# A hybrid encoder's RWKV-7 layer: gate weights scaled earlier, chunk matrices of all key tiles ahead of the gate products, and the triangular substitution started beside them

## The chip, the cores and the metric

The kernel runs on one core of one Trainium2 chip. The metric is the device time of one execution in microseconds, the median of several runs. A core has five engines with instruction streams of their own: TensorE (PE, with weight loads as PEld), VectorE (DVE), ScalarE (ACT), GpSimd (POOL) and SyncE (SP, which here issues the DMA transfers). They wait for one another by semaphores, and each runs its own stream in order.

## What is computed

The reference is a trunk of two layers over one sequence of 512 tokens with 1024 features. Layer 0 mixes tokens by a short gated convolution, layer 1 by RWKV-7; each is followed by a squared-ReLU MLP, with RMS norms and a modulation by a conditioning vector. The change lies in the RWKV-7 mixer:

```
xr, xw, xk, xv, xa, xg = h[None] + xx[None] * mu[:, None, None, :]
r, k, v = jnp.einsum('nbsd,nde->nbse', jnp.stack([xr, xk, xv]), w_rkv)
w = -jax.nn.softplus(-(w0 + jnp.tanh(xw @ w1) @ w2)) - 0.5
a = jax.nn.sigmoid(a0 + (xa @ a1) @ a2)
g = jax.nn.sigmoid(xg @ g1) @ g2
kk = heads(k * k_k)
kk = kk / jnp.maximum(jnp.sqrt(jnp.sum(kk * kk, axis=-1, keepdims=True)), 1e-12)
k = k * (1 + (a - 1) * k_a)
decay = jnp.exp(-jnp.exp(heads(w)))
y = _wkv7_scan(rh, decay, kh, vh, -kk, kk * ah)
...
out = ((y + bonus).reshape(bsz, seq, d).astype(h.dtype) * g) @ w_o
```

The scan runs token by token in the reference. The kernel cuts the sequence into chunks of 64 tokens; in a chunk the recurrence needs the inverse of a triangular matrix for each head (16 heads, 8 chunks), which is found by substitution.

## The kernel before, in words

Activations are kept transposed, 128 features on the partitions and 512 tokens along the free axis, so the 1024 features make eight tiles (KB). A product with a large weight matrix is done with the weights split into a high and a low part in a narrower format, as three matmuls per block of 128 features (`passes`, L171 to L173), 24 for one output tile. A weight block is loaded by SP (`raw`, L136), cast on ACT (L131), and the rest is subtracted on DVE (L132). DVE, ACT, POOL and SP instructions are put in order by the framework's scheduler; the order of PE is the order in which the code is written (`MANUAL`). In the RWKV layer it is written out as a string, `PLAN` (L34), each letter of which calls a function (`parts`, L833):

- K, `key_tile`: 24 matmuls for one tile of the keys; ACT then copies the tile (L602) and squares it (L604), and the norms' products on PE (L608) are kept back until `f` or a later step. The first three key tiles are done ahead of the plan.
- f: the norms' products that were kept back; n, `norms_now`: root, maximum and reciprocal of the norms so far (L625 to L629).
- W, `second_product`: four matmuls (L683) for the decay and the in-context rate of a tile, with tanh and scaling on ACT (L687 to L689). The prediction calls them decay products.
- s, `scaled`: a running sum of the decay along each chunk on DVE (L715), two exponentials on ACT (L717, L718), the norms repeated over the head's 64 rows by POOL (`repeat_norms`, L620), four transposes of them on PE (L723), and on DVE the scaled vectors (L726, L729, L730, L732, L734), with one product on POOL (L733).
- c, `chunk_matrix`: 16 pairs of small matmuls (L756) of two scaled vectors of the tile, a copy on ACT (L758) and a store to DRAM (L759).
- l: the loads of the gate's first weights (L547, L549) and their scaling on POOL (`gate_scale`, four times L533, one memset L556). L, `gate_lora`: three matmuls of these weights with the normed input (L634, L635, L674). a, G, A: what turns their sum into the gate's input (L793 is its last matmul).
- X, `xr_mix`: one tile of the input of the receptance. B, `chunk_back`: the loads of the chunk matrices (L746) for the substitution. U: the loads of the gate's second weights.

Behind the plan comes a loop of eight r tiles (L1256, 24 matmuls each, with the gates' second products and, in `beside_tile`, L1244, the mixes for the values and the steps of the substitution). The substitution has 30 steps of two DVE operations (L859, L861) over all heads and chunks at once. Its result is stored and read back in another layout by `inverted` (L863), with the tiles of `turn_tiles` (L847) beside it; then come the value tiles and the recurrence over the chunks, whose PE products L966, L982 and L997 wait for copies and products such as L922 (ACT) and L1033 (DVE).

Of the kernel before, what the change touches and what calls it, by code (L numbers as in the profile page):

```python
# [13 lines left out]
ALU = mybir.AluOpType  # L14
# [19 lines left out]
PLAN = "TfffffnWWsKWscfWKscfWscKWscfnWscWUsclscLLcBXXLLXXLLXXLLXXaGA"  # L34
NVEARLY, NTAIL = 2, 2
# [19 lines left out]
def trunk(ctx: ExitStack, tc: tile.TileContext, x_in, vec_in, c_in, ada0, ada, cin_a, wmain,  # L55
# [593 lines left out]
    with tc.manual_schedule(engines=MANUAL):  # L649
# [55 lines left out]
        def scaled():  # L705
# [27 lines left out]
            G.tensor_tensor(m, m, ei, op=ALU.mult)  # L733
# [14 lines left out]
        def chunk_matrix():  # L748
# [10 lines left out]
            nc.sync.dma_start(sc1.rearrange("(j g r) s t -> (r s) j g t", j=KB, r=2)[:, j], ab)  # L759

# [72 lines left out]
        parts = dict(f=lambda: flush(1), K=key_tile, T=first_out, n=norms_now, q=repeat_now,  # L833
# [11 lines left out]
        X2 = Xs[0]  # L845
# [9 lines left out]
        def substitute(t, tm):  # L855
            w = 31 - t
            sh = [P, 2, t, w]
            tv = tm[:, :2 * t * w].rearrange("p (q s c) -> p q s c", q=2, s=t)
            V.tensor_tensor(tv, X2[:, :, :t, t:t + 1].broadcast_to(sh), X2[:, :, t:t + 1, t + 1:].broadcast_to(sh),  # L859
                            op=ALU.mult)  # L860
            V.tensor_tensor(X2[:, :, :t, t + 1:], X2[:, :, :t, t + 1:], tv, op=ALU.add)  # L861

        def inverted():  # L863
            nc.sync.dma_start(sc2.rearrange("q p s t -> p q s t"), X2)
# [370 lines left out]
        for q in range(2):  # L1235
            G.affine_select(out=X2[:, q], in_=X2[:, q], pattern=[[-1, 32], [1, 32]], compare_op=ALU.is_gt, fill=0.0,
                            base=0, channel_multiplier=0)
            G.memset(X2[:, q].rearrange("p s t -> p (s t)")[:, 0:1024:33], 1.0)
        work = lambda t: 150 + 2 * t * (31 - t)
        steps, tm = list(range(30, 0, -1)), tmp()  # L1240
        total, subst = [sum(map(work, steps))], [0]
        nr = KB - done["R"]

        def beside_tile(i, mixes):  # L1244
            while len(xv) < mixes:
                xv.append(pair())
                mix(3, len(xv) - 1, FULL, *xv[-1])
            while steps and subst[0] + work(steps[0]) / 2 < total[0] * (i + 1) / (nr + NVEARLY - NTAIL):
                t = steps.pop(0)
                substitute(t, tm)  # L1250
                subst[0] += work(t)
                if not steps:
                    inverted()

        side = chain(*(v_tile(j) for j in range(KB)), x_back(), o_part(0), o_part(1), o_part(2))
        for i in range(nr):  # L1256
# [7 lines left out]
            if i == nr - 1:  # L1264
                turn_tiles()
# [113 lines left out]
```

## Time and profile before

| what | value |
|---|---|
| median of 3 runs | 1392.74 us (1389.88 to 1393.55) |
| profiled execution | 1391.49 us |
| its span in the trace | 1389.8 us |
| mean granted PE clock | 0.966 |
| PE busy | 1316.7 us (95%) |
| DVE busy | 838.3 us (60%) |
| ACT busy | 553.7 us (40%) |
| POOL busy | 163.2 us (12%) |

The durations in this document come from the profiled execution; its span is what the trace covers, and the execution's own time is 1.7 us longer. Shares of busy time are means over a program with many stages; the change concerns the stretch from about 625 us, where the plan begins, to about 806 us, where the recurrence over the chunks has begun. A wait in the profile is the idle time of an engine ahead of an instruction, put down to the instruction that released it. For a group of instructions in one row, the time is that of the group.

### The profile page before, as it was taken

How to read it: one execution, taken by the hardware profiler on the slowest of the kernel's cores; microseconds unless marked ns; L12 is line 12 of the kernel's file. 1: busy time of each engine (PE TensorE's matmuls, PEld its weight loads, DVE VectorE, ACT ScalarE, POOL GpSimd, SP SyncE). 2: the span in 40 equal slices, each digit the busy share in tenths (PEclk: the TensorE clock that was granted, in tenths of full speed). 3: DMA queues.
4: the chain of work that ended last, by engine and by line, in shares of the span. 5: the costliest groups of instructions: out<-in, count | busy, mean ns of one | idle time of the engine just before them, and what ended most of it. 6: DMA issues, size and time to landing. Idle time of an engine off the chain costs nothing.

```text
span 1389.8 us, 20232 instructions
## 1 busy us (share of the span) xinstructions
PE 1316.7 (95%) x8182; PEld 1080.1 (78%) x8182; DVE 838.3 (60%) x1233; ACT 553.7 (40%) x943; POOL 163.2 (12%) x175
## 2 busy tenths in 40 slices
PE   6899999999999999899599899999889999999997
PEld 3688889888888888887458677776678888888886
DVE  6996667756747565727669735465584344343445
ACT  3243334323233234547554557674344232232331
POOL 2300020000000003513311123232310000000000
PEclk7999999999999999998799999999999999999999
DMA  8466532635636355202445603321122223222231
GB/s 326 147 230 251 185 121 107 247 132 195 244 137 257 135 191 188 107 16 69 152 76 185 151 30 116 122 101 39 47 91 74 93 93 105 91 101 96 91 107 61
DMA packets 83392, 184.44 MB, mean 133 GB/s; under 512 B 35329, under 2 KB 37633, under 8 KB 83298
## 3 DMA queue, kind: packets, MB, share of 16 engines
q1 hardware_dynamic: 83298, 183.14, 38.6%
q8 instruction: 64, 1.05, 0.3%
q14 instruction: 30, 0.25, 0.1%
HBM read 168.44 MB, written 13.63 MB: 131 GB/s over the span
## 4 chain that ended last, share of the span: by engine, by line
PE 45%; ACT 3%; DVE 2%; issue 1%; POOL 0%; DVEq 0%; ACTq 0%
PE ps L171 12%; PE ps L173 12%; PE ps L172 11%; PE ps L982 1%; ACT b L1004 1%; PE ps L1060 1%; PE ps L1027 1%; PE ps L1096 1%; PE ps L1079 1%; PE ps L634 1%; PE ps L635 1%; PE ps L1091 1%; PE ps L674 0%; PE ps L1016 0%; PE ps L1120 0%
## 5 line engine op out<-in xcount | busy, mean ns | idle before, releaser
L171 PE MATMUL ps<-b,w 128*128 128x512 f32 (+1 forms) x1486 | 573.6, 386 | 1.2 <-ACT w L131 0.7
L173 PE MATMUL ps<-b,w 128*128 128x512 f32 (+1 forms) x1486 | 566.1, 381 | 2.2 <-POOL w L132 1.3
L172 PE MATMUL ps<-b,w 128*128 128x512 f32 (+1 forms) x1486 | 566.5, 381 | 0.0
L131 ACT CAST w<-raw 128x1024 fp32r<-128x1024 f32 x176 | 185.1, 1053 | 460.5 <-PE ps L172 432.1
L171 PEld LDWEIGHTS ps<-b,w 128*128 128x128 f32 x1486 | 282.7, 190 | 57.6 <-issue 3.2
L173 PEld LDWEIGHTS ps<-b,w 128*128 128x128 f32 x1486 | 282.7, 190 | 56.1 <-POOL w L132 1.8
L172 PEld LDWEIGHTS ps<-b,w 128*128 128x128 f32 x1486 | 282.8, 190 | 49.7
L132 DVE TENSOR_TENSOR w<-raw,w 128x1024 fp32r<-128x1024 f32 x172 | 211.8, 1232 | 144.5 <-ACT w L131 139.4
L205 DVE CUSTOM_DVE_ANT_0 cj<-b,cj,vec 128x1024 f32<-128x1024 f32 x96 | 137.9, 1436 | 10.8 <-DMA b<-in_ada 10.3
L302 DVE SCALAR_TENSOR_TENSOR b<-ps,mod,b 128x512 f32<-128x512 f32 (+1 forms) x84 | 56.4, 672 | 121.6 <-PE ps L173 121.2
L131 ACT CAST b<-t 128x512 fp32r<-128x512 f32 (+1 forms) x113 | 66.2, 591 | 114.3 <-DVE t L347 80.9
L132 DVE TENSOR_TENSOR b<-t,b 128x512 fp32r<-128x512 f32 x97 | 66.4, 692 | 26.7 <-ACT b L131 26.6
L302 DVE SCALAR_TENSOR_TENSOR xy<-ps,mod,xy 128x512 f32<-128x512 f32 x32 | 24.0, 750 | 62.1 <-PE ps L173 62.1
L256 ACT ACTIVATE b<-t,mod 128x256 fp32r<-128x256 f32 (+2 forms) x56 | 29.4, 537 | 56.0 <-DVE t L255 51.6
L171 PE MATMUL ps<-b,b 128*128 128x256 f32 (+1 forms) x152 | 47.3, 318 | 1.2 <-ACT b L256 1.1
L347 DVE TENSOR_TENSOR t<-t 128x512 f32<-128x512 f32 x64 | 43.5, 685 | 7.3 <-ACT t L346 7.3
L433 PE MATMUL ps<-b,b 128*128 128x512 f32 x168 | 40.6, 396 | 6.9 <-ACT b L256 6.9
L231 DVE TENSOR_TENSOR t<-t,t 128x256 f32<-128x256 f32 (+1 forms) x47 | 41.7, 886 | 7.8 <-ACT t L230 7.1
L172 PE MATMUL ps<-b,b 128*128 128x256 f32 (+1 forms) x152 | 45.0, 297 | 0.6 <-POOL b L132 0.6
L173 PE MATMUL ps<-b,b 128*128 128x256 f32 (+1 forms) x152 | 44.7, 295 | 0.0
L433 PEld LDWEIGHTS ps<-b,b 128*128 128x128 f32 x168 | 30.9, 188 | 16.9 <-ACT b L256 10.6
L533 POOL TENSOR_TENSOR b<-b,vec 128x512 f32<-128x512 f32 (+2 forms) x4 | 4.7, 1195 | 325.5 <-DMA b<-in_l 323.9
(208 smaller groups left out, 1321.3 us busy)
## 6 DMA issues: line engine op xcount, KB each, us to landing
raw<-in_wmain SPq DMA_DIRECT2D x185, 512.0 KB, 3.3
b<-in_ada SPq DMA_DIRECT2D x96, 512.0 KB, 5.7
sp<-b SPq DMA_DIRECT2D x8, 512.0 KB, 2.7
b<-sp SPq DMA_DIRECT2D x8, 512.0 KB, 4.6
b<-in_cin_a SPq DMA_DIRECT2D x8, 448.0 KB, 6.9
b<-in_x SPq DMA_DIRECT2D x8, 256.0 KB, 6.1
xs<-b SPq DMA_DIRECT2D x8, 256.0 KB, 2.3
sc<-t SPq DMA_DIRECT2D x8, 256.0 KB, 2.8
```

Source lines behind the costliest of these rows:

```text
L131: A.copy(dst_hi, src)
L132: return (eng or V).tensor_tensor(dst_lo, src, dst_hi.bitcast(F32), op=ALU.subtract)
L171: PE.matmul(dst, whi, ahi, start=start, stop=False)
L172: PE.matmul(dst, whi, alo, start=False, stop=False)
L173: return PE.matmul(dst, wlo, ahi, start=False, stop=stop)
L205: return V.tensor_tensor_reduce(junk, w, cb, 1.0, vv(f"ab{l}{v}", m), ALU.mult, ALU.add, mods[l, v][:, m:m + 1])
L231: V.tensor_tensor(acc[:, sl], acc[:, sl], t[:, :w], op=ALU.add)
L256: A.activation(hi[:, sl], t[:, :w], AF.Identity, bias=sh[:, k:k + 1])
L302: V.scalar_tensor_tensor(x[m][:, sl], pt[:, sl], gt[:, m:m + 1], x[m][:, sl], op0=ALU.mult, op1=ALU.add)
L347: V.tensor_tensor(r, r, r, op=ALU.mult)
L433: PE.matmul(pts[i], a[:, i * P:(i + 1) * P], h[k][b], start=k == 0 and a is whi and not b, stop=k == KB - 1 and b == 1)
L634: PE.matmul(pt[:, sl], w0, h[k][:, sl], start=start, stop=False)
```

## The change

In the plan, the loads and the scaling of the gate weights (l) stand first; the norms (f) stand right behind their key tile; each tile's chunk matrix (c) stands behind its own scaled step (s), with all eight ahead of the first gate product (L); and a new letter u runs steps of the substitution (a share of 0.06 of its work each) between the gate products. The product L733 goes from POOL to DVE. What is left of the substitution is spread over the first seven r tiles instead of the first eight, the store of its result is issued right behind its last step, and the tiles that are read back, and the reading, come behind the r loop.

```diff
--- before.py
+++ after.py
@@ -31,8 +31,8 @@
 POSTW = 0.742
 STATY = 0.155
 BENG = None
-PLAN = "TfffffnWWsKWscfWKscfWscKWscfnWscWUsclscLLcBXXLLXXLLXXLLXXaGA"
-NVEARLY, NTAIL = 2, 2
+PLAN = "TlfffffnWWsWsKfcWscWsKfcWscKfncWscWsUcscLLBXXLXXLXXLuXXLuLLuaGAu"
+NVEARLY, NSUB, USUB = 2, 7, 0.06
 G2ENG = None
 NMORE = 2
 TA = (0, 1), (0, 1), (0, 1)
@@ -730,7 +730,7 @@
             V.scalar_tensor_tensor(bt, al, -0.5, bt, op0=ALU.mult, op1=ALU.mult)
             al3 = al.rearrange("p (c t) -> p c t", t=64)
             V.tensor_tensor(al3[:, :, 1:], al3[:, :, 1:], e3[:, :, :63], op=ALU.mult)
-            G.tensor_tensor(m, m, ei, op=ALU.mult)
+            V.tensor_tensor(m, m, ei, op=ALU.mult)
             V.tensor_tensor(kt, kt, m, op=ALU.mult)
 
         Xs = []
@@ -757,6 +757,33 @@
             ab = tmp().rearrange("p (c t) -> p c t", t=64)
             A.copy(ab, pab)
             nc.sync.dma_start(sc1.rearrange("(j g r) s t -> (r s) j g t", j=KB, r=2)[:, j], ab)
+
+
+        work = lambda t: 150 + 2 * t * (31 - t)
+        steps, tms = list(range(30, 0, -1)), []
+        total, subst = sum(map(work, steps)), [0.0]
+
+        def substitute(t):
+            X2, tm = Xs[0], tms[0]
+            w = 31 - t
+            sh = [P, 2, t, w]
+            tv = tm[:, :2 * t * w].rearrange("p (q s c) -> p q s c", q=2, s=t)
+            V.tensor_tensor(tv, X2[:, :, :t, t:t + 1].broadcast_to(sh), X2[:, :, t:t + 1, t + 1:].broadcast_to(sh),
+                            op=ALU.mult)
+            V.tensor_tensor(X2[:, :, :t, t + 1:], X2[:, :, :t, t + 1:], tv, op=ALU.add)
+
+        def advance(part):
+            if not tms:
+                tms.append(tmp())
+                for q in range(2):
+                    X = Xs[0][:, q]
+                    G.affine_select(out=X, in_=X, pattern=[[-1, 32], [1, 32]], compare_op=ALU.is_gt, fill=0.0, base=0,
+                                    channel_multiplier=0)
+                    G.memset(X.rearrange("p s t -> p (s t)")[:, 0:1024:33], 1.0)
+            while steps and subst[0] + work(steps[0]) / 2 / total < part:
+                t = steps.pop(0)
+                substitute(t)
+                subst[0] += work(t) / total
 
         g2, gahl = [], []
 
@@ -830,7 +857,7 @@
             A.copy(gt_, pg)
             nc.sync.dma_start(gs[:, j], gt_)
 
-        parts = dict(f=lambda: flush(1), K=key_tile, T=first_out, n=norms_now, q=repeat_now,
+        parts = dict(u=lambda: advance(subst[0] + USUB), f=lambda: flush(1), K=key_tile, T=first_out, n=norms_now, q=repeat_now,
                      W=second_product, L=gate_lora, X=xr_mix, l=lambda: (gate_loads(), gate_scale()), U=gate_loads2, G=gate_weights, a=gate_part, A=gate_in, s=scaled, c=chunk_matrix,
                      R=r_tile, p=spill, g=gates, b=lambda: chunk_back(1),
                      B=lambda: chunk_back(0), w=lambda: w_raw(wst["nraw"] + 1))
@@ -842,7 +869,6 @@
         TT = []
         s1u = sc1.rearrange("(g u r) s t -> s r g u t", r=2, g=4)
         s2u = sc2.rearrange("q (g u r) s t -> q s r g u t", r=2, g=4)
-        X2 = Xs[0]
 
         def turn_tiles():
             TT.extend(big((P, 16, 64), F32) for _ in range(4))
@@ -852,16 +878,8 @@
                     G.memset(TT[g][o + 32:o + 64, :, 0:32], 0.0)
                     nc.sync.dma_start(TT[g][o:o + 32, :, 32:], s1u[0:32, par, g, :, 32:])
 
-        def substitute(t, tm):
-            w = 31 - t
-            sh = [P, 2, t, w]
-            tv = tm[:, :2 * t * w].rearrange("p (q s c) -> p q s c", q=2, s=t)
-            V.tensor_tensor(tv, X2[:, :, :t, t:t + 1].broadcast_to(sh), X2[:, :, t:t + 1, t + 1:].broadcast_to(sh),
-                            op=ALU.mult)
-            V.tensor_tensor(X2[:, :, :t, t + 1:], X2[:, :, :t, t + 1:], tv, op=ALU.add)
-
         def inverted():
-            nc.sync.dma_start(sc2.rearrange("q p s t -> p q s t"), X2)
+            turn_tiles()
             for g in range(4):
                 for q in range(2):
                     for par in range(2):
@@ -1232,25 +1250,16 @@
             yield XWAIT
 
 
-        for q in range(2):
-            G.affine_select(out=X2[:, q], in_=X2[:, q], pattern=[[-1, 32], [1, 32]], compare_op=ALU.is_gt, fill=0.0,
-                            base=0, channel_multiplier=0)
-            G.memset(X2[:, q].rearrange("p s t -> p (s t)")[:, 0:1024:33], 1.0)
-        work = lambda t: 150 + 2 * t * (31 - t)
-        steps, tm = list(range(30, 0, -1)), tmp()
-        total, subst = [sum(map(work, steps))], [0]
-        nr = KB - done["R"]
+        nr, sub0 = KB - done["R"], subst[0]
 
         def beside_tile(i, mixes):
             while len(xv) < mixes:
                 xv.append(pair())
                 mix(3, len(xv) - 1, FULL, *xv[-1])
-            while steps and subst[0] + work(steps[0]) / 2 < total[0] * (i + 1) / (nr + NVEARLY - NTAIL):
-                t = steps.pop(0)
-                substitute(t, tm)
-                subst[0] += work(t)
+            if steps:
+                advance(sub0 + (1 - sub0) * (i + 1) / NSUB)
                 if not steps:
-                    inverted()
+                    nc.sync.dma_start(sc2.rearrange("q p s t -> p q s t"), Xs[0])
 
         side = chain(*(v_tile(j) for j in range(KB)), x_back(), o_part(0), o_part(1), o_part(2))
         for i in range(nr):
@@ -1261,9 +1270,8 @@
             if j < 2:
                 He[j] = big(dt=F32)
                 nc.sync.dma_start(He[j][0:64], ar[j][0:64])
-            if i == nr - 1:
-                turn_tiles()
             beside_tile(i, KB * (i + 1) // nr)
+        inverted()
         for i in range(NVEARLY):
             while len(vdone) <= i:
                 next(side)
```

The orders below are those of one engine's instructions before and in the changed kernel; names such as b, t, ps are buffers with their numbers.

On POOL, at the start of the plan, before (L620 repeats the norms of one tile, L733 is the product of the scaled step):

```order
L620 TENSOR_SCALAR t_4769<-rn 128x512
L620 TENSOR_SCALAR t_4781<-rn 128x512
L733 TENSOR_TENSOR t_4784<-t_4784,t_4772 128x512
L620 TENSOR_SCALAR t_4845<-rn 128x512
L733 TENSOR_TENSOR t_4848<-t_4848,t_4836 128x512
L620 TENSOR_SCALAR t_4933<-rn 128x512
```

and now:

```order
L556 MEMSET b_4729 128x256
L620 TENSOR_SCALAR t_4779<-rn 128x512
L533 TENSOR_TENSOR b_4727<-b_4726,vec 128x1024
L533 TENSOR_TENSOR b_4729<-b_4729,omu 128x8x32
L533 TENSOR_TENSOR b_4726<-b_4726,omu 128x1024
L533 TENSOR_TENSOR b_4729<-b_4729,vec 128x8x32
L620 TENSOR_SCALAR t_4791<-rn 128x512
L620 TENSOR_SCALAR t_4821<-rn 128x512
```

The memset and the four scalings of the gate weights (L556, L533) now stand here, and the second repeated norm (t_4791) stands behind them; L733 has left POOL.

On PE, at the end of the first key tile of the plan (L173 is its last matmul, L608 the products of its norms, L723 the transposes of repeated norms), before:

```order
L173 MATMUL ps_4791<-b_4232,w_4683 128x512
L683 MATMUL ps_4825<-b_4713,b_4029 128x512
L683 MATMUL ps_4825<-b_4713,b_4030 128x512
L683 MATMUL ps_4826<-b_4713,b_4068 128x512
L683 MATMUL ps_4826<-b_4713,b_4069 128x512
L723 MATMUL ps_4840<-ident,t_4781 128x128 x4
L756 MATMUL ps_4855<-b_4755,b_4694 64x64 x16
L608 MATMUL ps_4362<-blk,b_4822 128x2 x4
```

and now:

```order
L173 MATMUL ps_4831<-b_4232,w_4683 128x512
L608 MATMUL ps_4362<-blk,b_4862 128x2 x4
L756 MATMUL ps_4869<-b_4765,b_4694 64x64 x16
L683 MATMUL ps_4889<-b_4713,b_4029 128x512
L683 MATMUL ps_4889<-b_4713,b_4030 128x512
L683 MATMUL ps_4890<-b_4713,b_4068 128x512
L683 MATMUL ps_4890<-b_4713,b_4069 128x512
L723 MATMUL ps_4904<-ident,t_4821 128x128 x4
```

The norms' products moved from behind the decay products, the transposes and the chunk matrix to right behind the key tile. On ACT at the same place (L131 is the cast of a weight block, L602 and L604 are the key tile's copy and square) the cast stands ahead of copy and square, as it did before:

```order
L718 ACTIVATE b_4775<-b_4775 128x512
L720 COPY eend_4714<-b_4775 128x8
L131 CAST w_4994<-raw_4860 128x1024
L602 COPY b_4862<-ps_4831 128x512
L604 ACTIVATE b_4862<-ps_4831,vec 128x512
L758 COPY t_4886<-ps_4869 128x512
```

On PE, from the transposes of the sixth key tile (tile 5) to the first gate product (L634), before:

```order
L723 MATMUL ps_5123<-ident,t_5116 128x128 x4
L756 MATMUL ps_5138<-b_4973,b_4706 64x64 x16
L683 MATMUL ps_5158<-b_4713,b_4029 128x512
L683 MATMUL ps_5158<-b_4713,b_4030 128x512
L683 MATMUL ps_5159<-b_4713,b_4068 128x512
L683 MATMUL ps_5159<-b_4713,b_4069 128x512
L723 MATMUL ps_5179<-ident,t_5128 128x128 x4
L756 MATMUL ps_5194<-b_5057,b_4822 64x64 x16
L723 MATMUL ps_5229<-ident,t_5184 128x128 x4
L756 MATMUL ps_5242<-b_5112,b_4920 64x64 x16
L634 MATMUL ps_5262<-b_4183,b_5214 128x512
```

and now:

```order
L723 MATMUL ps_5153<-ident,t_5146 128x128 x4
L756 MATMUL ps_5168<-b_5033,b_4862 64x64 x16
L683 MATMUL ps_5188<-b_4713,b_4029 128x512
L683 MATMUL ps_5188<-b_4713,b_4030 128x512
L683 MATMUL ps_5189<-b_4713,b_4068 128x512
L683 MATMUL ps_5189<-b_4713,b_4069 128x512
L723 MATMUL ps_5203<-ident,t_5158 128x128 x4
L756 MATMUL ps_5224<-b_5142,b_5000 64x64 x16
L723 MATMUL ps_5249<-ident,t_5208 128x128 x4
L756 MATMUL ps_5262<-b_5194,b_5106 64x64 x16
L634 MATMUL ps_5282<-b_4183,b_4726 128x512
```

Before, the chunk matrices (L756) there were those of tiles 4, 5 and 6, each behind the transposes of the tile after it; now they are those of tiles 5, 6 and 7, each behind the transposes of its own tile.

## Rows read from the trace of the kernel before

**Rows 1.** The table by windows: stretch, length, busy us of each engine, PE clock, DMA

```profile
640.60:642.80 2.20, 2.20 (x7) 1.81 (x7) 2.20 (x3) 0.82 (x3) 1.62 (x2) 0.50 0.45 119
625.08:713.34 88.26, 70.55 (x466) 49.32 (x466) 62.67 (x74) 58.25 (x101) 26.93 (x26) 0.84 0.40 102
778.70:806.40 27.70, 20.13 (x359) 18.61 (x358) 11.70 (x16) 17.69 (x45) 5.59 (x8) 0.82 0.61 154
```

**Rows 2.** Waits of PE from 625 to 714: us in total, times, longest

```profile
PE ps L756 <- DVE b L732: 5.8, 2, 4.3
PE ps L634 <- POOL b L533: 5.7, 1, 5.7
PE ps L723 <- POOL t L620: 2.7, 1, 2.7
PE ps L756 <- ACT b L688: 1.7, 1, 1.7
PE ps L793 <- ACT t L778: 1.3, 1, 1.3
```

**Rows 3.** The timeline of POOL: start us, us, engine, line, operation

```profile
626.33 1.21 POOL L620 TENSOR_SCALAR t<-rn 128x512 f32<-128x512 f32 x2 [26.91 <-PE ps L683]
...
683.52 1.90 POOL L533 TENSOR_TENSOR b<-b,vec 128x1024 f32<-128x1024 f32 x1 [1.59 <-DMA b<-in_g]
685.38 2.91 POOL L533 TENSOR_TENSOR b<-b,omu 128x256 f32<-128x256 f32 x2
688.25 0.61 POOL L533 TENSOR_TENSOR b<-b,vec 128x256 f32<-128x256 f32 x1
```

**Rows 4.** The timeline of SP's DMA issues near 620

```profile
619.81 0.33 SPq L136 DMA_DIRECT2D raw<-in_wmain  x1
```

**Rows 5.** The timeline of ACT behind the second key tile

```profile
648.49 1.05 ACT L131 CAST w<-raw 128x1024 fp32r<-128x1024 f32 x1 [1.73 <-PE ps L172]
649.45 0.58 ACT L602 COPY b<-ps 128x512 f32<-128x512 f32 x1
649.92 0.69 ACT L604 ACTIVATE b<-ps,vec 128x512 f32<-128x512 f32 x1
```

**Rows 6.** The timeline of PE at the same place

```profile
648.29 0.40 PE L173 MATMUL ps<-b,w 128*128 128x512 f32 x1
...
650.67 1.05 PE L608 MATMUL ps<-blk,b 128*128 128x2 f32 x8 [0.46 <-ACT b L604]
```

**Rows 7.** The timeline of DVE, key tiles 5 to 7

```profile
671.88 0.75 DVE L726 SCALAR_TENSOR_TENSOR b<-b,vec,ps 128x512 f32<-128x512 f32 x1 [1.80 <-PE ps L723]
672.54 0.68 DVE L729 SCALAR_TENSOR_TENSOR b<-b,t 128x512 f32<-128x512 f32 x1
673.15 0.68 DVE L734 TENSOR_TENSOR b<-b,t 128x512 f32<-128x512 f32 x1
...
674.54 1.56 DVE L732 TENSOR_TENSOR b<-b 128x504 f32<-128x504 f32 x1
676.02 1.21 DVE L715 TENSOR_TENSOR_SCAN b<-cmask,b 128x512 f32<-128x512 f32 x1
...
679.87 0.68 DVE L732 TENSOR_TENSOR b<-b 128x504 f32<-128x504 f32 x1
...
683.53 2.43 DVE L732 TENSOR_TENSOR b<-b 128x504 f32<-128x504 f32 x1
```

**Rows 8.** The timeline of PE: decay products at the lower and higher clock

```profile
640.68 2.05 PE L683 MATMUL ps<-b,b 128*128 128x512 f32 x4
...
651.58 1.19 PE L683 MATMUL ps<-b,b 128*128 128x512 f32 x4
```

**Rows 9.** Waits from 778 to 807, all engines

```profile
ACT w L131 <- DMA raw<-in_wmain: 9.9, 1, 9.9
...
PEld ps L997 <- ACT b L922: 3.0, 1, 3.0
PE ps L997 <- DVE b L1033: 2.7, 1, 2.7
```

## The prediction

> **What bounds the kernel now.** I read the page first: TensorE (PE) is busy for most of the span, so time is won or lost only where PE stops or runs slowly. Then the table by windows. The change touches the stretch from 625.08 to 713.34, from the end of the first key tiles to the first gate sum. There PE is busy for 70.55 of 88.26 us, with a mean granted clock of 0.84 of full speed; the same table gives 0.82 for the start of the chunk recurrence, where the results of the substitution are first used [rows 1]. These two stretches are where anything can happen. Between them, in the r tiles, the substitution runs on DVE beside a PE that has its weights, so moving its steps there buys nothing by itself.
>
> Then the waits of PE. From 625 to 714 they are 5.8 us for the chunk matrix on the DVE chain (L756 on L732), 5.7 for the first gate product on POOL's scaling of the gate weights (L634 on L533), 2.7 for a transpose on a repeated norm (L723 on L620), 1.7 for a chunk matrix on ACT and 1.3 for the gate sum [rows 2], and 0.46 for the norms' product [rows 6]: **17.7 us of stops**. The change removes the 5.7 at once: the loads and the scaling come before the first remaining key tile. The question is what the new order of PE puts in its place.
>
> **The change part by part.** All sums are against the profiled execution, 1391.49 us, whose span is 1389.8; the median of the runs, 1392.74, is 1.25 above it.
>
> *A: gate weights scaled early.* POOL now holds the first repeated norm, then the four L533, then the second repeated norm. Before, two repeated norms took 1.21 us together from 626.33, 0.61 each; the four L533 took 1.90 + 2.91 + 0.61 = 5.42 [rows 3]. So the second is done at 626.33 + 1.21 + 5.42 = 633.0 at the earliest. The gate loads don't make that later by much: in SP's order they stand right behind a weight load that was issued at 619.81 [rows 4], six microseconds ahead of POOL. PE needs the second repeated norm for the transposes of tile 1, which now stand ahead of the first key tile. It gets there at about 631.3, an estimate: the stretch starts at 625.08, and three decay products (1.19 to 2.05 us each by the clock [rows 8], so 3.6 to 6.2) and the transposes of tile 0 lie ahead; I choose the later end, since the clock is low in a part of them. That makes 1.7 us. But POOL and DVE slow each other here: L732 took 2.43 us while POOL ran its 1.90 us L533, against 0.68 alone, and 1.56 beside a POOL product [rows 7]. DVE runs splits and scans of 1.21 us in the new place (a scan's row: [rows 7]). I take three microseconds of mutual holding, the second repeated norm at 636.0, and a **stop of 4.7 us**; the ends are 1.7 (no holding) and 6.0.
>
> The Trainium skill, page "SBUF — State Buffer", section "Who interferes with whom", says that DVE and GpSimd share one pair of ports under an exclusive lock, held for a whole instruction. It speaks against scaling on POOL in the busiest stretch of DVE; by it the stop would be near 6.0 and the time about 1403.3; by POOL's rows alone it would be 1.7 and the time about 1399.0. L732's 2.43 against 0.68 us agrees with it.
>
> *B: norms right behind the key tile.* Behind a key tile's 24 matmuls come a copy and a square on ACT, and the norms need the square. Before, the second key tile ended at 648.29 + 0.40 = 648.69 [rows 6]. ACT began a weight cast of 1.05 us at 648.49, then copy and square of 0.58 and 0.69; the square began at 649.92 [rows 5], and the norms ran at 650.67, 1.98 us behind the key tile's end, with other products in PE's order between to fill that time, and a wait of 0.46 [rows 6]. Now the norms are PE's next instruction, and the cast still stands ahead of copy and square on ACT. PE stands for about 2.0 us, three times: **6.0 us**. The chunk matrix and the decay product behind the norms don't depend on them, but PE runs in order. The ends are 1.4 (0.46 each, as before) and 6.0.
>
> *C: the chunk matrices of the last tiles.* Before, each of the last tiles' chunk matrices stood behind the transposes of the next tile, and the last one behind gate products, so a tile's DVE chain ran beside the next tile. Now tiles 5, 6 and 7 have their own transposes and their own chunk matrix side by side; the last decay product stands behind tile 5's chunk matrix and covers nothing. The chain from transposes to chunk matrix is L726 (672.54 - 671.88 = 0.66), a scan that the order puts between, 676.02 on (1.21 long, about 1.15 to the next start), four operations of 0.60 each (L729, L733, L730, L734; 673.15 - 672.54 = 0.61 from start to start, and L733 taken like L734, which has its form), and L732 of 0.68 [rows 7]: 0.66 + 1.15 + 2.4 + 0.68 and 0.1 for the two hand-overs (an estimate) = 5.0 for tiles 5 and 6, and about 3.8 for tile 7, which has no scan behind it. **13.8 us**, about what the two old waits on L732, the norm's wait and the wait on L533 were together (5.8 + 5.7 + 2.7 = 14.2). The gate products that are now ready could have filled this, but they come after it in PE's order. Moving L733 from POOL to DVE is in the chain already: one 0.60 more there, and no wait across engines. For the other tiles the key tiles' matmuls cover it. The 2.7 us stop of the transposes on their norm gets a chunk matrix as cover beside the decay product; I count what is left of it at nothing, 0.7 at most.
>
> New stops: 4.7 + 6.0 + 13.8 + 1.3 (the gate sum, unchanged) = 25.8, less 17.7: **+8.1 us**.
>
> *D: the clock.* After a stop PE runs on at the lower of its levels: from 640.60 to 642.80, behind the 1.7 us stop on ACT, the granted clock is 0.50, that is 1.2 GHz, with PE busy all the time [rows 1], and the four decay-product matmuls there take 2.05 us; in the next tile, with no stop ahead, they take 1.19 [rows 8]. The loss of 0.86 on these four is about half of such a stretch (an estimate from these rows): 1.7 us a stop. The change makes four stops among the key tiles (A, and B three times) and removes one (the 1.7 on ACT): 3 x 1.7 = **+5.1 us**. The last tiles run low before and after. Ends: 0 (the level holds through 2 us) and 9.
>
> *E: the tail.* Before, the store of the inverted blocks sits in SP's queue ahead of weight loads; a weight load keeps ACT's cast waiting 9.9 us (L131), ACT's copy L922 behind it comes late, and PE stops at L997 for 2.7 on DVE L1033, which waits for the same data [rows 9]. Now the store goes out at the seventh of eight r tiles and its reloads behind the loop. I take the 2.7 as gone: **-2.7 us**, between 0 and -4.4.
>
> The substitution steps that start in the gate products cost DVE time in a stretch where it is busy for 62.67 of 88.26 us [rows 1] and PE does not wait for it in the gate products; their cover is the rest of the gate products, and the price without it would be a mix of xr that comes late by a few operations of the 0.68 kind [rows 7]. I cost them at nothing.
>
> **Sum:** +8.1 + 5.1 - 2.7 = +10.5, so 1391.49 + 10.5 = **1402.0 us**.
>
> **Rivals.** *The clock holds* through stops of 2.0 us: then D is gone, 1402.0 - 5.1 = 1396.9. For it: behind the second key tile the 0.46 stop leaves the decay products at 1.19 [rows 6, 8]; against it: 1.7 was enough to lower it [rows 1, 2].
>
> *Worse*: POOL is held to the 6.0 end of A (+1.3), the tail stays (+2.7), and each stop's low stretch costs more, towards the 9 of D (+3.9): 1402.0 + 7.9 = 1409.9. For it: PE's clock stays low for most of the last tiles, 0.84 in the mean [rows 1].
>
> *Faster*: the work is reordered so that the covers suffice: the norms' wait stays at 0.46 as ACT takes copy and square first, the second repeated norm is early enough, and only the 5.7 on L533 and the 2.7 on L997 vanish: 1391.49 - 8.4 = 1383.1. It decides at the place of the last tiles: PE's stops there must sum to under 14.2 - 5.7 = 8.5, that is under 2.8 a tile, where the chain that I read is 3.8 to 4.9; against it, too, the cast stands ahead of copy and square in ACT's order.
>
> That the change doesn't do what it says is excluded: the orders of PE, POOL and DVE show each move.
>
> **How the numbers follow.** 0.43 for the forecast (1398 to 1407), 0.20 for the clock that holds, 0.19 for worse, 0.14 for faster, 0.04 for mishaps that no row shows. About 0.3%, 4.2 us, is what a measurement of this kernel can tell from no change. Faster: 0.14 and a little: 0.15. Same: half of the clock case, whose 1396.9 stands at the bound, 0.10. Slower: 0.75. The range leaves out the faster case and the mishaps, and takes in the bounds of A, B and D: 1392 to 1414.
>
> **What would show it.** In the profile after: no wait of L634 on L533; a wait of L723 on L620 near 632 of 2 to 6 us; three waits of L608 on the square of about 2 us, with decay products (L683) at 2.05 behind them; waits of L756 on L732 (or L734) of 4 to 5 us for each of the last three tiles; L997's wait on L1033 gone. If the waits of L608 and of the last L756 are under 1 and 2.8 us, the prediction is wrong and the kernel is faster.

## The result, and the profile after

The changed kernel takes **1403.09 us** (median of 5 runs, 1398.41 to 1405.45) against 1392.74 before: the ratio is 1.0068, with a 95% interval of 1.0042 to 1.0094. It is slower by 10.3 us in the medians; the forecast was 1402.0. The profiled execution shown here took 1405.45 us, with a span of 1403.7.

The table by windows from the first decay product of the stretch to the gate sum (this and all such rows below: start and end, length, then busy us of PE, PEld, DVE, ACT and POOL with their instructions, granted PE clock, DMA share, GB/s), after:

```profile
625.92:728.64 102.72, 76.16 (x466) 53.13 (x466) 66.61 (x98) 58.90 (x100) 18.89 (x17) 0.78 0.32 81
```

It answers to the row of 88.26 us in [rows 1]. The stretch is 14.5 us longer. PE does the same 466 matmuls and is busy 5.6 us longer (76.16 against 70.55), with a granted clock of 0.78 instead of 0.84: the clock's part. It stands still for 26.6 us instead of 17.7: 8.9 us of stops. Behind the gate sum the changed kernel needs 675.1 us (1403.7 - 728.64), the one before 676.5. The remaining 0.8 us lie ahead of the stretch (625.92 against 625.08). There the profiled executions of this study differ by up to 4.7 us (the stretch begins between 621.31 and 625.97 us), so below the lengths of the stretch are compared beside the medians.

The waits of PE from 615 to 760, after (us in total, times, longest), which answer to [rows 2]:

```profile
PE ps L756 <- DVE b L732: 14.5, 3, 5.5
PE ps L608 <- ACT b L604: 6.8, 4, 2.0
PE ps L723 <- POOL t L620: 4.7, 1, 4.7
PE ps L820 <- ACT t L805: 1.3, 1, 1.3
```

L820 is the gate sum (L793 before). Its wait is as long as before; the other three are new or longer, and no first gate product waits for L533 any more. One of the four waits on the norms, 0.8 us, lies ahead of the stretch, as it does in other kernels of this study. Where the waits stand is read from PE's timeline after (start, us, line, idle time ahead in brackets):

```profile
636.07 1.12 PE L723 MATMUL ps<-ident,t 128*128 128x128 f32 x4 [4.74 <-POOL t L620]
...
646.18 1.05 PE L608 MATMUL ps<-blk,b 128*128 128x2 f32 x8 [1.99 <-ACT b L604]
647.16 1.97 PE L756 MATMUL ps<-b,b 64*64 64x64 f32 x32
649.06 1.88 PE L683 MATMUL ps<-b,b 128*128 128x512 f32 x4
...
661.50 1.05 PE L608 MATMUL ps<-blk,b 128*128 128x2 f32 x8 [1.98 <-ACT b L604]
662.48 1.15 PE L756 MATMUL ps<-b,b 64*64 64x64 f32 x32
...
673.91 1.37 PE L608 MATMUL ps<-blk,b 128*128 128x2 f32 x8 [1.98 <-ACT b L604]
675.22 1.98 PE L756 MATMUL ps<-b,b 64*64 64x64 f32 x32
...
685.50 1.97 PE L756 MATMUL ps<-b,b 64*64 64x64 f32 x32 [5.45 <-DVE b L732]
...
695.38 1.97 PE L756 MATMUL ps<-b,b 64*64 64x64 f32 x32 [5.05 <-DVE b L732]
...
702.42 1.98 PE L756 MATMUL ps<-b,b 64*64 64x64 f32 x32 [4.03 <-DVE b L732]
```

Behind the first stop of the norms the chunk matrix takes 1.97 us and the decay product 1.88; without a stop ahead they take 1.15 and 1.19 in the same trace. Behind the second stop, as long as the first, the chunk matrix takes 1.15; behind the third 1.98. The windows behind the second stop and from the third through the last tiles (the granted clock is the third number from the end, 1.00 and 0.56):

```profile
662.00:674.00 12.00, 10.02 (x102) 8.17 (x102) 6.78 (x9) 7.02 (x13) 0.00 (x0) 1.00 0.41 131
674.00:704.30 30.30, 15.78 (x156) 13.18 (x156) 14.28 (x23) 13.99 (x24) 1.78 (x3) 0.56 0.39 127
```

POOL's timeline after, which answers to [rows 3]:

```profile
627.16 0.62 POOL L620 TENSOR_SCALAR t<-rn 128x512 f32<-128x512 f32 x1 [28.28 <-DVE rn L629]
627.74 2.86 POOL L533 TENSOR_TENSOR b<-b,vec 128x1024 f32<-128x1024 f32 x1
630.57 2.46 POOL L533 TENSOR_TENSOR b<-b,omu 128x256 f32<-128x256 f32 x2
633.00 1.53 POOL L533 TENSOR_TENSOR b<-b,vec 128x256 f32<-128x256 f32 x1
634.49 3.55 POOL L620 TENSOR_SCALAR t<-rn 128x512 f32<-128x512 f32 x3
```

The four scalings take 6.85 us (2.86 + 2.46 + 1.53) instead of the 5.42 that they took in their old place, and the second repeated norm begins only at 634.49. DVE pays too: its two scans beside them (L715) take 3.77 us, where one alone takes 1.21 [rows 7].

### The profile page after: what moved, and what is told of

It reads as the page before. It is cut to its first block, busy times and chain, and to the rows that moved or that the text cites. A ratio compares the mean times of both kernels' runs of the same rounds, so it can differ in the third digit from the quotient of the medians.

```text
span 1403.7 us, 20206 instructions
## 1 busy us (share of the span) xinstructions
PE 1323.4 (94%) x8182; PEld 1084.4 (77%) x8182; DVE 837.6 (60%) x1241; ACT 554.1 (39%) x943; POOL 155.2 (11%) x167
## 4 chain that ended last, share of the span: by engine, by line
PE 85%; DVE 7%; ACT 5%; issue 1%; POOL 1%; DMA 0%; SPq 0%; DVEq 0%; ACTq 0%; POOLq 0%
PE ps L171 24%; PE ps L172 23%; PE ps L173 23%; DVE cj L205 2%; DVE t L231 2%; PE ps L1000 1%; ACT b L1022 1%; PE ps L1045 1%; ACT w L131 1%; PE ps L634 1%; PE ps L635 1%; PE ps L1078 1%; PE ps L608 1%; PE ps L756 1%; PE ps L1114 1%
## 5 line engine op out<-in xcount | busy, mean ns | idle before, releaser
L173 PE MATMUL ps<-b,w 128*128 128x512 f32 (+1 forms) x1486 | 565.4, 380 | 2.2 <-POOL w L132 1.3
L131 ACT CAST w<-raw 128x1024 fp32r<-128x1024 f32 x176 | 184.9, 1052 | 464.2 <-PE ps L172 447.6
L173 PEld LDWEIGHTS ps<-b,w 128*128 128x128 f32 x1486 | 281.9, 190 | 55.8 <-POOL w L132 1.8
L132 DVE TENSOR_TENSOR w<-raw,w 128x1024 fp32r<-128x1024 f32 x172 | 211.9, 1232 | 154.0 <-ACT w L131 148.4
L131 ACT CAST b<-t 128x512 fp32r<-128x512 f32 (+1 forms) x113 | 66.1, 590 | 114.8 <-DVE t L347 80.9
L132 DVE TENSOR_TENSOR b<-t,b 128x512 fp32r<-128x512 f32 x97 | 66.4, 692 | 26.5 <-ACT b L131 26.4
L173 PE MATMUL ps<-b,b 128*128 128x256 f32 (+1 forms) x152 | 44.8, 296 | 0.0
L533 POOL TENSOR_TENSOR b<-b,vec 128x512 f32<-128x512 f32 (+2 forms) x4 | 6.8, 1710 | 323.9 <-DMA b<-in_l 323.9
```

The source lines that it names most:

```text
L131: A.copy(dst_hi, src)
L132: return (eng or V).tensor_tensor(dst_lo, src, dst_hi.bitcast(F32), op=ALU.subtract)
L173: return PE.matmul(dst, wlo, ahi, start=False, stop=stop)
```

## The experiments

Each is told with its edit against the kernel named. For all but two the edit is in the string that sets PE's order. A ratio always compares with the kernel before on the same chip. Differences between the medians of two experiments can lie across chips, whose medians of the kernel before lie between 1392.74 and 1394.43 us.

**The gate weights' scaling behind the second scaled step.** Against the changed kernel:

```diff
-PLAN = "TlfffffnWWsWsKfcWsc...
+PLAN = "TfffffnWWsWslKfcWsc...
```

> The changed kernel with the letter l behind the second scaled step, so that POOL repeats the norms of tiles 0, 1 and 2 before it scales the gate weights. Theory (the early scaling holds the second repeated norm back): the changed kernel's 4.7 us stop of the transposes (L723) on L620 near 632 goes, at most 0.5 is left, and the low clock behind it too; the other stops stay: 1403.1 - 4.7 - 1.7 = 1396.7. Rival (the stop is only a place where PE waits for something that would be late anyway, DVE's scans or a weight block): another stop of 3 to 5 us stands near 632 to 640 and the time stays within 1401 to 1405.

Measured: 1398.6 us, ratio to before 1.0038 (1.0024 to 1.0052); the stretch is 95.8 us, 7.0 less than in the changed kernel. The wait on L620 is gone. Of its 4.7 us a part comes back at the next place: the first key tile's norms wait 3.16 instead of 1.99, as ACT is still busy with the steps that used to fall into the old stop.

```profile
639.72 1.87 PE L608 MATMUL ps<-blk,b 128*128 128x2 f32 x8 [3.16 <-ACT b L604]
```

So the stop is the early scaling's, as the theory has it, and its net worth is 4.5 us in the medians where 6.4 was expected.

**The norms later.** Against the changed kernel, three times:

```diff
-...WsKfcWscWsKfcWscKfncWsc...
+...WsKcWfscWsKcWfscKcWfnsc...
```

> The changed kernel with f not right behind the key tile but behind the chunk matrix and the decay product that follow it. Theory (ACT's cast, copy and square stand between key tile and norms, and other products fill that time): the three stops of L608 of 2.0 us go to under 0.3 each, 6.0 us, and the low clock behind the first and the third goes with them, 3.4 us; but the last norms now have nothing behind them before the scaled step, so the transposes stop for about 3 us on L620 as in the kernel before: 1403.1 - 9.4 + 3 = 1396.7. Rival without the clock's part: 1400. Rival that the chunk matrix waits there instead of the norms (its DVE chain not done when the key tile ends): stops of L756 of over 1 us behind the key tiles, and no gain.

Measured: 1394.23 us, ratio 1.0012 (0.9999 to 1.0025); the stretch is 93.9 us, 8.8 less. The two longest of PE's waits from 610 to 830 in this kernel:

```profile
PE ps L756 <- DVE b L732: 13.4, 3, 5.4
PE ps L723 <- POOL t L620: 8.7, 2, 4.6
```

All waits of L608 on the key tiles of the plan are gone, and no chunk matrix waits in their place. The second wait on L620, 4.0 us, is the one that was expected at about 3. PE is busy 70.59 us in the stretch instead of 76.16: the clock's part is 5.6 us here, larger than the 3.4 that I gave it. The time falls by 8.9 us in the medians where 6.4 was expected.

**The stops filled.** Against the changed kernel, two products of constants between each key tile and its norms (they compute nothing that is used):

```diff
+        def fill():
+            pd = bank()
+            for _ in range(2):
+                PE.matmul(pd, ones, cmask, start=True, stop=True)
...
+        parts = dict(d=fill, ...
-...WsWsKfcWscWsKfcWscKfncWsc...
+...WsWsKdfcWscWsKdfcWscKdfncWsc...
```

> The changed kernel with two extra 128x128x512 fp32 products into a bank that nobody reads, between each key tile of the plan and its norms, 1.7 us at the higher clock in a stop of 2.0 us; they compute nothing that is used. Theory (PE's stop itself lowers the clock): the decay products behind the first and the third of these stops take 1.2 instead of 1.9 to 2.1 us, and the time falls by about 3.4 us to 1399.7 although no wait is removed. Rival (the clock falls there for another reason, or the stops cost only their length): the rows stay at 1.9 to 2.1 and the time at 1403.

Measured: 1398.97 us, ratio 1.0042 (1.0027 to 1.0057). PE's timeline at the first of the three places:

```profile
640.73 1.88 PE L863 MATMUL ps<-cmask,ones 128*128 128x512 f32 x4
642.87 1.05 PE L608 MATMUL ps<-blk,b 128*128 128x2 f32 x8 [0.26 <-ACT b L604]
643.85 1.15 PE L756 MATMUL ps<-b,b 64*64 64x64 f32 x32
644.93 1.21 PE L683 MATMUL ps<-b,b 128*128 128x512 f32 x4
```

The chunk matrix takes 1.15 instead of 1.97 us and the decay product 1.21 instead of 1.88, with the data still as late as before. At the third place it is the same. At these two places the stop itself therefore lowered the clock, and PE's idle time is not its whole price; why the second stop of the same length did not, the runs don't show. The stretch is 100.3 us, 2.5 less than in the changed kernel; a part of the gain is given back at the first of the last tiles, where the chunk matrix now waits 6.73 us instead of 5.45. The medians differ by 4.1, 3.4 was expected; the 1.6 beyond the stretch is within the executions' spread.

**Gate products as cover of the last tiles.** Against the changed kernel, the first is the edit, and the next experiment takes the early steps (u) out of it too:

```diff
-...KfncWscWsUcscLLBXXLXXLXXLuXXLuLLuaGAu
+...KfncWsLLcWsLLUcsLLcBXXLXXLuXXuXXuaGAu
+...KfncWsLLcWsLLUcsLLcBXXLXXLXXXXaGA
```

> The changed kernel with two gate products (L) between the transposes and the chunk matrix of each of the tiles 5, 6 and 7; nothing else moves, two gate products are left for behind. Theory (the last tiles' DVE chain stands bare on PE): the 14.5 us of L756 on L732 go to under 1, and PE's clock in the last tiles is higher than the 0.56 of the changed kernel, worth 2 to 4 us more: 1403.1 - 13.5 - 3 = 1386.6. Rival (the gate products covered the mixes of xr on DVE, which now are bare): a new wait of up to 5 us of the gate sum or of the first r tile on DVE or ACT, 1391 to 1392.

Measured: 1398.5 us, ratio 1.0037 (1.0025 to 1.005). The waits on L732 fell from 14.5 to 0.3 us, as expected, and 13.3 came up at the gate sum, far more than the rival's 5. Three of the waits from 700 to 722:

```profile
PE ps L820 <- ACT t L805: 13.3, 1, 13.3
ACT b L131 <- DVE t L501: 8.8, 4, 6.5
DVE t L771 <- POOL xs L780: 6.1, 1, 6.1
```

Followed back: the gate sum waits for ACT's L805, which stands behind casts of the xr mixes (L131), which wait for DVE's mixes (L501), which stand behind the first substitution step (L771) in DVE's order, and that step waits 6.1 us for POOL's triangular mask (L780), itself waiting for the chunk matrices to come back from DRAM.

> The kernel of the third experiment (gate products as cover of the last tiles) without the early steps of the substitution: all 30 steps run beside the r tiles. Theory (in the third experiment the first step stands in DVE's order ahead of the mixes of xr and waits 6.1 us for the chunk matrices' way through DRAM and for POOL, and ACT's L805 stands behind the mixes' casts): the gate sum's stop falls from 13.3 to about 7, what is left is the mixes themselves, about 11 us of DVE work of which little is covered, and the time falls by 6 to 1392.5. Rival (the mixes alone make the stop): the stop stays at 12 or more and the time at 1398.

Measured: 1387.81 us, ratio 0.995 (0.9936 to 0.9964), 10.7 us less where 6 was expected; 8.6 of them lie in the stretch (85.96 against 94.54 us). The gate sum's wait:

```profile
PE ps L820 <- ACT t L805: 4.6, 1, 4.6
```

The early steps, harmless while gate products covered them, cost most of the gain as soon as these are spent elsewhere.

**Without the early steps, else as changed.** Against the changed kernel, every u is left out of the string.

> The changed kernel without its early steps of the substitution; all 30 run beside the first seven r tiles, the rest stays. Theory (the early steps are worth nothing: PE has gate products and then weights all that time, and DVE's 4.35 us wait for the chunk matrices' way through DRAM lies behind gate products): the stretch to the gate sum stays at 102 to 103 us and the time at 1401 to 1405. Rival (the early steps save time in the tail or beside the r tiles): 1406 to 1410. Rival (DVE's wait delays the mixes of xr): 1398 to 1400.

Measured: 1400.77 us, ratio 1.0056 (1.0035 to 1.0076), the stretch 101.9 us against 102.7. In the changed kernel DVE waits 4.3 us at the same step, with gate products on PE all that time. They buy nothing and cost nothing that these runs can tell.

**The product on DVE alone.** Against the kernel before:

```diff
-            G.tensor_tensor(m, m, ei, op=ALU.mult)
+            V.tensor_tensor(m, m, ei, op=ALU.mult)
```

> The kernel before with one edit of the change alone: the product L733 on DVE. Theory (it costs one 0.6 us operation in the chains that stand bare, two of them, and takes a hand-over between engines and POOL's holding of DVE away): the stretch from the first decay product to the gate sum is 88.3 us before and 87 to 89.5 with it, the time 1392 to 1394.5. Rival (POOL's product holds up DVE's L732, 1.56 instead of 0.68 us, and the chain waits for POOL): the two stops of L756 on L732 fall from 5.8 to about 3 and the stretch to 85 us, 1390.

Measured: **1387.42 us**, ratio 0.9952 (0.9936 to 0.9967). The theory was wrong, and the rival too small and in the wrong place: the two stops on L732 fell only from 5.8 to 5.0. The stretch is 83.3 us, 4.9 less than before, 3.0 of it stops and 1.9 busy time of PE (68.64 against 70.55); the medians differ by 7.0, and where the other 2.1 lie no trace shows. DVE's timeline before, at the first tile of the plan:

```profile
633.03 0.69 DVE L729 SCALAR_TENSOR_TENSOR b<-b,t 128x512 f32<-128x512 f32 x1 [0.29 <-ACT t L728]
634.91 1.09 DVE L734 TENSOR_TENSOR b<-b,t 128x512 f32<-128x512 f32 x1 [1.19 <-POOL t L733]
635.92 0.68 DVE L730 SCALAR_TENSOR_TENSOR b<-b,b 128x512 f32<-128x512 f32 x1
636.52 1.21 DVE L132 TENSOR_TENSOR w<-raw,w 128x1024 fp32r<-128x1024 f32 x1
637.66 0.67 DVE L732 TENSOR_TENSOR b<-b 128x504 f32<-128x504 f32 x1
```

and in this experiment:

```profile
632.87 0.69 DVE L729 SCALAR_TENSOR_TENSOR b<-b,t 128x512 f32<-128x512 f32 x1 [0.29 <-ACT t L728]
633.48 0.68 DVE L733 TENSOR_TENSOR t<-t,t 128x512 f32<-128x512 f32 x1
634.09 0.69 DVE L730 SCALAR_TENSOR_TENSOR b<-b,b 128x512 f32<-128x512 f32 x1
634.69 0.68 DVE L734 TENSOR_TENSOR b<-b,t 128x512 f32<-128x512 f32 x1
635.29 0.68 DVE L732 TENSOR_TENSOR b<-b 128x504 f32<-128x504 f32 x1
```

With the product on POOL, DVE waits 1.19 us for it, L734 takes longer, and a weight subtraction stands ahead of L732 in DVE's order; L732 begins 2.4 us later than with the product on DVE. The chunk matrix's stop of 1.7 us near 638, which the trace before put down to ACT's L688, is gone with it, and the low clock behind it: the decay products there take 1.17 us instead of 2.05. The chunk matrix before, then in this experiment, and L688 in this experiment:

```profile
638.48 1.15 PE L756 MATMUL ps<-b,b 64*64 64x64 f32 x32 [1.73 <-ACT b L688]
...
636.30 1.15 PE L756 MATMUL ps<-b,b 64*64 64x64 f32 x32
...
637.26 0.74 ACT L688 ACTIVATE b<-b,half 128x512 f32<-128x512 f32 x1
```

Here the chunk matrix starts ahead of L688, so it does not need it. Before, L732 ended at 638.33 and the chunk matrix began at 638.48: L732 was what it waited for.

**The order of before, with the rest of the change.** The changed kernel with the old string.

> The changed kernel with the PLAN of before: what is left of the change is L733 on DVE, the substitution over the first seven r tiles, and the store, the memsets and the reloads behind it in their new places. Theory (the new order of PE is the whole loss, the tail gains): the stretch to the gate sum is back at 88 us with its old stops, L1015 and L1013 wait about 2 us less than L997 did before, and the time is 1390 to 1392. Rival (a part of the loss lies behind the gate sum, in the later reloads): 1395 to 1398.

Measured: **1384.8 us**, ratio 0.9928 (0.9915 to 0.994). The stretch is 83.7 us, close to that of the experiment before:

```profile
625.57:709.30 83.73, 69.03 (x465) 47.89 (x466) 59.59 (x82) 57.86 (x100) 13.98 (x18) 0.85 0.42 107
```

The rest of the kernel behind it is 673.8 us (1383.1 - 709.30) against 677.2 there: the old 2.7 us wait of L997 on L1033 is gone, and 1.1 us (L1013 on L1051) stands in its place. So the string alone makes the loss: 1403.1 - 1384.8 = 18.3 us in the medians, 19.0 in the stretch (102.72 - 83.73). The product's move is a gain. That the tail is one, too, is read from the traces; in the times the intervals of these two experiments overlap.

**The early scaling in the old order.** Against the experiment before:

```diff
-...nWWsKWscfWK...nWscWUsclscLL...
+...nWWsKWslcfWK...nWscWUscscLL...
```

> The changed kernel with the order of before (the sixth experiment), and the gate weights' loads and scaling moved behind the third scaled step, with two repeated norms ahead of the scaling on POOL. Theory (the early scaling is good where no norm waits behind it): the 5.8 us stop of L634 on L533 goes, and the other stops stay: 1384.8 - 5.8 = 1379. Rival (POOL's scaling holds DVE's chain or the third repeated norm): a new stop of 2 to 5 us near 640 and 1381 to 1385.

The place is behind the second scaled step (the expectation says the third); three repeated norms then stand ahead of the scaling. Measured: 1383.31 us, ratio 0.9923 (0.9903 to 0.9944): no different from 1384.8. The 5.8 us stop on L533 is gone, and the rival came: rows of POOL, DVE and PE, in this order, in this kernel:

```profile
629.90 4.31 POOL L533 TENSOR_TENSOR b<-b,omu 128x256 f32<-128x256 f32 x2
...
632.44 2.32 DVE L729 SCALAR_TENSOR_TENSOR b<-b,t 128x512 f32<-128x512 f32 x1
...
638.05 1.40 PE L756 MATMUL ps<-b,b 64*64 64x64 f32 x32 [2.19 <-DVE b L732]
639.38 1.87 PE L608 MATMUL ps<-blk,b 128*128 128x2 f32 x8
```

The stretch in this kernel:

```profile
624.82:708.31 83.49, 72.37 (x465) 50.68 (x466) 61.88 (x82) 58.40 (x100) 17.78 (x18) 0.83 0.40 100
```

The pair of scalings takes 4.31 us instead of 2.91 [rows 3], DVE's L729 2.32 instead of 0.69, and the chunk matrix waits 2.2 us. PE's stops in the stretch fall by 3.6 us (11.1 against 14.7), but PE is busy 3.3 us longer (72.37 against 69.03): 2.9 us of that lie ahead of the transposes that wait for a repeated norm, at 667.53 there and 663.19 in the experiment before (37.97 against 35.07). The early stop of 2.2 us stands in that part; it gave back most of the gain through the clock.

**All covers.** Against the changed kernel, the whole string:

```diff
+PLAN = "TfffffnWWsWslKcWfscWsKcWfscKcWfnWLsLLcXXsLLUcXXsLLcXXBLaAXXG"
```

> All that the experiments point to in one order: the scaling of the gate weights behind the second scaled step, norms behind the products that follow their key tile, all of the eight gate products spread as cover (one ahead of tile 5's transposes, two behind the transposes of each of the tiles 5, 6 and 7, one last), two mixes of xr behind each of these tiles, no early substitution. Theory: of the changed kernel's stretch of 102.7 us the stops of A, B and C go with their low clock (6.6 + 9.4 + 16), and the mixes, which the scheduler puts between the operations of the chains, give back about 5: 76 us, 1376 to 1380. Rival (DVE is the bound then, with 15 us of chains and 11 of mixes beside 26 us of PE work): stops of L756 and of the gate sum of over 10 us in sum, 1386. If it is over 1392, the kernel before stays the best order.

Measured: **1375.29 us** (1373.47 to 1382.11; the profiled execution is one of the longer, 1381.24), ratio 0.9877 (0.9855 to 0.9899); the stretch is 75.7 us, as the theory has it. The stops of L756 and of the gate sum are 7.3 us in sum, not the rival's 10 and more (those of L756, then of the gate sum):

```profile
PE ps L756 <- DVE b L732: 5.4, 4, 2.2
PE ps L820 <- ACT t L805: 1.9, 1, 1.9
```

**The mixes behind the chains.** Against that:

```diff
-PLAN = "TfffffnWWsWslKcWfscWsKcWfscKcWfnWLsLLcXXsLLUcXXsLLcXXBLaAXXG"
+PLAN = "TfffffnWWsWslKWcfscWsKcWfscKcWfnWLsLLcsXXLLUcsXXLLcXXBLaAXXG"
```

> The kernel of the order with all covers, with the mixes of xr written behind the next tile's scaled step, so that the scheduler puts them behind a chain instead of into it, and with the first chunk matrix behind the decay product. Theory (the mixes inside the chains make the stops of L756, 5.4 us in four, and the first of these lowers the clock): the stops of L756 fall to 2 us or less and the stretch to the gate sum from 75.7 to 72 us: 1372. Rival (DVE's work is the bound there, wherever the mixes stand): the stops move to the gate sum and the first r tile, and the time stays at 1374 to 1377.

Measured: **1373.2 us** (1371.59 to 1374.32), ratio 0.9853 (0.9837 to 0.987), the lowest median of this study, 20.7 us below the runs of before beside it. Its interval overlaps that of the experiment before, so the times don't show that the second order is faster; only the stretch is shorter, 68.9 against 75.7 us in the one profiled execution of each. The edit has two parts, the mixes and the first chunk matrix, which were not run apart. Its windows and its waits of PE in the stretch:

```profile
621.31:690.25 68.94, 64.08 (x465) 43.93 (x466) 55.34 (x77) 54.26 (x95) 15.35 (x14) 0.96 0.36 106
```

```profile
PE ps L756 <- DVE b L732: 2.6, 3, 1.5
PE ps L820 <- ACT t L805: 1.9, 1, 1.9
PE ps L723 <- POOL t L620: 0.4, 1, 0.4
```

Against the changed kernel PE stands 4.9 us instead of 26.6 and is busy 64.1 instead of 76.2, with the same matmuls (one is missing from the trace). Not all of this is gained: behind the gate sum this kernel needs 679.7 us (1369.9 - 690.25), where the changed kernel with the order of before needs 673.8; two of the waits there are new, of L173 on L132 (1.0 us) and of L855 on L798 (0.8).

## Why the prediction was right, point by point

**The size.** 1402.0 was forecast and 1403.09 measured. In the stretch, stops of 25.8 us were forecast and 26.6 came; the clock was to cost 5.1 and cost 5.6. That the total came within 1.1 us is in part luck: executions of the changed kernel spread over 7.0 us (1398.41 to 1405.45), and the two profiled ones differ by 13.9 us in their spans (8.9 of stops, 5.6 of clock and 0.8 ahead of the stretch, less 1.4 behind it).

**A, the second repeated norm:** 4.7 forecast, 4.74 measured, PE arriving at 631.33 (636.07 - 4.74). The parts differ from my guess: the scalings grew by 1.4 us, the start was 0.8 later, and L620 itself ran at twice its time (3.55 us for three, 0.61 each before). The Trainium skill, page "SBUF — State Buffer", section "Who interferes with whom", has a DVE instruction with two SBUF inputs contend with a GpSimd instruction that reads SBUF, under an exclusive lock. By it I had put the stop near 6.0; 4.74 was measured. Its direction is borne out: in the experiment with the early scaling in the old order, L729 took 2.32 instead of 0.69 us beside a scaling.

**B, the norms:** 2.0 us each forecast; 1.99, 1.98 and 1.98 measured, and moving them showed the cause. **C, the last tiles:** 13.8 forecast, 14.5 measured, 5.45, 5.05 and 4.03 for the 5.0, 5.0 and 3.8 of the sum. Given gate products there, PE waited 0.3: the stops are the DVE chains with nothing on PE beside them.

**D, the clock:** the experiment with filled stops showed the mechanism, which the prediction had only from one place of the trace. Of the three stops of the norms two lowered the clock, not three; behind the second, the chunk matrix took 1.15. The last tiles, which the prediction left out since they "run low before and after", made up for it: from the third stop of the norms to the first gate products PE was busy for 19.6 us at a granted clock of 0.50, and for 11.5 in the last tiles and the first gate products before; at half speed that is 4.1 us more, an estimate from these two numbers. So the sum of D is near what was measured, but not by its parts. The 0.84 that the rival "worse" gives for the last tiles is the mean of the whole stretch [rows 1]; from 675 to 690 the clock before was 0.50. The rival in which the clock holds through 2.0 us was true of one stop in three, and falls as a whole.

**E, the tail:** 2.7 forecast; 1.4 us by the two profiled executions of the result, and by the two experiments that differ in it 3.4 behind the gate sum and 2.6 in the medians (1387.4 and 1384.8), whose intervals overlap. PE's wait for that product of DVE (L1033 before, L1051 now) did not vanish, as the prediction has it, but fell from 2.7 to 1.1 us, in the changed kernel too.

**The early steps at nothing:** right in this order of PE, and only there; the cover that I named, the gate products, is what makes it so. Its price without them, which I put at a few operations of 0.68 us, was too small by far: 8.6 us in the stretch, as the first step waits 6.1 us and the mixes stand behind it.

**The step that failed** is the sentence on L733: "one 0.60 more there, and no wait across engines". It gave the move no gain. In the old order the move alone is worth 4.9 us in the stretch and 7.0 in the medians (1394.4 to 1387.4); what it is worth in the new order no run shows. The sum came out right all the same, since it took off all old stops, the 1.7 us one "on ACT" among them, and booked their end to the new order. Part by part, the forecast was 13.2 us for the order (8.1 + 5.1), nothing for L733 and -2.7 for the tail. The runs show 18.3 for the order (19.0 in the stretch), and 9.6 given back by the other two together (1394.4 to 1384.8). The two numbers come from different chips and don't add up to the 10.3 us exactly.

**The rival "faster"** named the point that decides, under 2.8 us a tile. The last two experiments meet it, with gate products between transposes and chunk matrix: 3.3 and 0.4 us in the three last tiles together.

## What to carry to other kernels

Bringing work forward on one engine pays only where its instructions pass nobody that is waited for: look up what stands behind it on its queue, and which engine slows down beside it. When one group of products is the only cover that a stretch has, spend it between the producer's start and the consumer, not behind both. And read a stop of PE twice, once as idle time and once as the longer busy time of the same matmuls behind it.

## What the runs showed that was not expected

Eight products of 128x512 values on POOL, one a tile, cost more than their rows let see. They stood on an engine that is busy 12% of the time, with two waits of 2.4 us in sum put down to them, and 4.9 us of the stretch and 7.0 us of the median went with them. The stop of PE that went with them stood in the profile under ACT's L688: the delay had been passed on by DVE's own order.

The same 466 matmuls took PE between 64.1 and 76.2 us of busy time in these kernels, as the granted clock of the stretch went from 0.96 to 0.78.
